# The sample's tile normalised and projected ahead of the prompt's last two tiles, instead of as the last one of the stage

## The chip, the cores and the metric

The kernel runs on one core of one Trainium2 chip. The metric is the device time of one execution in microseconds (us); a median of several executions is given with the lowest and the highest. The engines are named as in the profile: PE is the matrix engine (PEld its weight loads), DVE the vector engine, ACT the scalar engine, POOL the GpSimd engine, and SP the engine whose queue issues every DMA of this kernel.

## What is computed

One layer of a streaming encoder runs over two streams: a prompt of 2048 rows (16 tiles of 128 rows, numbered 0 to 15) and a sample of 32 rows (tile 16). Cut to what matters here:

```python
def _layer(x, c, pos, past_k, past_v, h0, lw):
    mod = silu(c) @ w_ada + b_ada
    sh1, sc1, g1, sh2, sc2, g2 = split(mod, 6)
    h = rmsnorm(x, ln1_g) * (1 + sc1) + sh1
    proj = h @ w_in                            # 1024 -> q 512 | k 128 | v 128 | u 512
    q = rope(rmsnorm(q per head), pos); k = rope(rmsnorm(k per head), pos)
    attn = banded attention of q, k, v         # the sample also reads cached k, v
    ssm_y, h_last = s5(u, h0, ...)             # state space layer over all rows of a stream
    g = gelu(ssm_y); ssm_o = g * sigmoid(g @ glu_w + glu_b)
    x = x + g1 * (concat(rmsnorm(attn), rmsnorm(ssm_o)) @ w_out)
    h2 = rmsnorm(x, ln2_g) * (1 + sc2) + sh2
    return x + g2 * ((silu(h2 @ w_gate) * (h2 @ w_up)) @ w_down), k rows, v rows, h_last
```

Both streams use the same weights, with their own conditioning vector, positions and past. Matrices are split into a high and a low float32r part, and a product is the sum of three matmuls (high by high, high by low, low by high).

## The kernel before

The kernel has four stages. Stage A normalises every tile of 128 rows, transposes it and multiplies it by `w_in`; stage B does the state space groups and the first attention tiles; stage C the rest of attention, the output projection and the residual; the last stage, by far the longest, is the feed-forward part. The change lies in stage A.

The kernel's text is a set of Python generators that are stepped in turn. A scheduler then orders the instructions of each engine, with the order of the text as their priority and a simulated time line to tell when each is ready; so instructions of different generators come out interleaved, and more finely than the text has them. Each engine, and SP's queue of DMA issues, then runs its list in order.

Stage A is the loop at lines 853 to 866. It goes through the tiles in pairs, `p` = 0 to 8: tiles (0, 1), (2, 3) up to (14, 15), and then tile 16 alone. For each pair it steps the projection of its tiles (`proj_steps`), and with every step of that

- one step, or two, of `x_steps(p + 1)`, the normalisation of the pair after it,
- one step of `wg`, which loads and splits the q, k and v columns of `w_in`, as long as there are any,
- two times in three a step of `bg1`, the conditioning vectors of the later stages (`ada_blocks`, tiles `adw`, `adh`, `adl`, `adp`, `adr`),
- one step of `bg2`, the tables and matrices of the state space layer (`ssm_background`; tiles `et`, `etb` on POOL, `m`, `mt`, `bv`, `spl` on DVE, `sph` on ACT, `kb` and `pbv` on PE).

`x_steps(p)` (lines 266 to 285) takes the row tiles `xg` of its pair. ACT squares and sums each (written into `hl` as scratch), POOL makes the inverse root (`rs`, two instructions), ACT scales the rows. Then `norm_steps` goes through the 8 blocks of 128 columns, one step for each: PE transposes the block of both tiles (`tr`), ACT applies scale and shift (`hf`), ACT or DVE makes the high part (`hh`) and DVE the low part (`hl`; for the sample both parts lie in `hh`). These results have two sets of buffers, so `x_steps(p + 1)` can begin only when the projection of pair `p - 1` has read its last block. For a pair it issues 16 transposes, for the sample 8 of 32 columns. At its end it issues the loads of later row tiles (`x_load`; `xg` has three buffers).

`proj_steps(j)` (lines 831 to 839) first does the u columns (`u_steps`: `ub`, copied to `us` and stored to `u_d`). Tiles 0 to 5 (`LATE`) store their normalised tile to `hT_d`, and their q, k and v are done at the start of stage B (`deferred`, tiles `dh` and `dl`). For all others `qkv_steps` follows: `qp` (512 columns), `kp` (256 columns), rotation on DVE (`qkvo`, `rb`) with the last addition on POOL, the per-head norm (`sq`, `ms`), and the stores to `qkv_d`; tile 15 and tile 16 also store their k and v rows to outputs (line 815). A prompt tile has 48 matmuls of 512 columns and 24 of 256. The sample has its high and low parts side by side as one stationary operand of 64 columns, so it has 32 of 512 and 16 of 256, and its two halves are added on DVE by `fold` (lines 126 to 129: a copy and an addition, for `ub`, `qp` and `kp`). Its `fold` results go to `qf`, which takes a buffer of `xg`.

When the loop is done, stage B opens. `ssm_batch` (lines 932 to 945) loads u rows 0 to 1023 (`ur`), has ACT rearrange them (`us`), loads rows 1024 to 2047 into the same single buffer `ur`, and then the sample's rows. The group steps load their matrices (`sm`, `ec`), and PE transposes u (`up`, lines 963 and 964).

Of the kernel before, what the change touches and what calls it, by code (L numbers as in the profile page):

```python
# [23 lines left out]
NT = NPT + 1  # L24
# [23 lines left out]
FLO = 576  # L48
CST = 2
QY = 2  # L50
LATE = [0, 1, 2, 3, 4, 5]
TILES = [*range(8, NPT), *range(8), NPT]
UNITS = [4, 5, 6, 7, 0, 1, 2, 3, 8]
# [20 lines left out]
def hybrid_kernel(  # L74
# [25 lines left out]
    def act(out, a, func=AF.Copy, **kw):  # L100
        A.activation(out, a, func, **kw)  # L101

    def f(a):
        return a.bitcast(F32)
# [37 lines left out]
    kp_d = dram.tile([16, G, 256], F32, name="kp_d")  # L142
    hT_d = dram.tile([len(LATE), 2, 128, KD * 128], F32, name="hT_d")
    sd_d = dram.tile([12, 4, 128, 512], F32, name="sd_d")
# [14 lines left out]
    def rpow(out, ss, n, eps, scr):  # L159
        ts(P, scr, ss, 1.0 / n, eps)  # L160
        tt(P, out, scr, mhalf[0:scr.shape[0]].to_broadcast(list(scr.shape)), ALU.pow)
# [23 lines left out]
    def qbank(nm="qp"):  # L185
        return pqs.tile([128, 512], F32, tag="q", name=nm)
# [21 lines left out]
    def advance(g, n=1):  # L208
        for _ in range(n):
            if next(g, None) is None:  # L210
                return
# [26 lines left out]
    def norm_steps(xs, rcol, s, hs, n, scv, shv, getbank, tmp):  # L238

        nt = len(xs)  # L240
        if rcol is not None:
            for j in range(nt):
                act(xs[j][0:n], xs[j][0:n], scale=rcol[0:n, j:j + 1])
        yield 1
        for k in range(KD):
            pb = getbank([128, nt, 128])
            for j in range(nt):
                PE.transpose(pb[:, j, 0:n], xs[j][0:n, k * 128:(k + 1) * 128], ident[0:n, 0:n])
            hf = tmp([128, nt, n])
            act(hf, pb[:, :, 0:n], AF.Identity, scale=scv[:, k, s:s + 1], bias=shv[:, k, s:s + 1])  # L250
            split(hs[0][:, 0:nt, k, 0:n], hs[1][:, 0:nt, k, 0:n], hf, V if k % 2 else A, V)
            yield 1

    xt, ht = {}, {}

    def x_load(j):
        if j >= NT:
            return
        x = px.tile([128, D], F32, tag="xg", name="xg", bufs=3)
        if j < NPT:  # L260
            SP.dma_start(x, x_prompt[0, j * 128:(j + 1) * 128])
        else:
            SP.dma_start(x[0:DEC], x_sample[0])
        xt[j] = x

    def x_steps(p):
        tl = [j for j in (2 * p, 2 * p + 1) if j < NT]
        xs = []
        hs = [px.tile([128, 2, KD, 128], F32R, tag=t, name=t, bufs=2) for t in ("hh", "hl")]
        rs = px.tile([128, 3, 2], F32, tag="rs", name="rs", bufs=2)  # L270
        for i, j in enumerate(tl):
            x = xt.pop(j)
            n = 128 if j < NPT else DEC
            act(hs[1][0:n, i].rearrange("p k n -> p (k n)"), x[0:n], AF.Square, accum_out=rs[0:n, 0, i:i + 1])
            xs.append(x)
            ht[j] = (hs[0][:, i], hs[1][:, i])
        if n < 128:
            ht[j] = (hs[0][:, 0, :, 0:2 * n], None)
            hs = [hs[0][:, :, :, i * n:i * n + n] for i in range(2)]
        nt = len(tl)  # L280
        rpow(rs[0:n, 1, 0:nt], rs[0:n, 0, 0:nt], D, EPS, rs[0:n, 2, 0:nt])
        yield 1
        yield from norm_steps(xs, rs[:, 1], 0 if n == 128 else 1, hs, n, sc1, sh1, tbank, partial(px.tile, dtype=F32, tag="hf", name="hf", bufs=3))
        for j in tl:
            x_load(j + 3)

    def ada_vectors(i, row, getbank):
        which, half = divmod(i, 2)
# [11 lines left out]
    def ada_first():  # L300
# [4 lines left out]
        for k in range(KD):  # L305
            if k == 3:
                for i in range(4):
                    SP.dma_start(rows[i][4:5], b_ada[0:1, i * 512:(i + 1) * 512])
            if k == 7:
                x_load(0)  # L310
                x_load(1)
                advance(xg)
            for i in (2, 3, 0, 1):
                wf = wq_tile("wqh" if k % 2 else "wql", 2 * (k // 2 % 2) * 2 + i, F32)[:, 0:512]
                wh = pz.tile([128, 512], F32R, tag="adfh", name="adfh", bufs=2)
                wl = pz.tile([128, 512], F32R, tag="adfl", name="adfl", bufs=2)
                SP.dma_start(wf, w_ada[0, k * 128:(k + 1) * 128, i * 512:(i + 1) * 512])
                split(wh, wl, wf, A, V)
                mm(acc[i], cst[:, k], wh, k == 0, False)
                mm(acc[i], cst[:, k], wl, False, k == KD - 1)  # L320
# [400 lines left out]

    wur = [px.tile([128, 4, 512], F32, tag=t, name="wur", bufs=2) for t in ("hh", "hl")]
    xg = x_steps(0)
    bg2 = ssm_background()
    ada_first()
# [33 lines left out]
    def product(dst, h, wh, wl, o, w):  # L759
        for k in range(KD):  # L760
            mm3(dst, h[0][:, k], h[1] and h[1][:, k], wh[k][:, o:o + w], wl[k][:, o:o + w], k == 0, k == KD - 1)
            if k % 2 and (w == 512 or k == 3) and k < KD - 1:
                yield 1
# [54 lines left out]
    def u_steps(j, h):  # L818
        n = 128 if j < NPT else DEC
        ub = qbank() if j in LATE else psu.tile([128, 512], F32, tag="ub", name="ub")  # L820
        yield from product(ub if n == 128 else ub[0:2 * n], h, [wuh[:, k] for k in range(KD)],
                           [wul[:, k] for k in range(KD)], 0, 512)
        yield 1
        us = psx.tile([128, 512], F32, tag="us", name="us")[0:n]
        if n < 128:
            fold(us, ub)
        else:
            cp(A, us, ub)
        SP.dma_start(u_d[j * 128:j * 128 + n], us)

    def proj_steps(j):
        h = ht.pop(j)
        if j in LATE:
            for i in range(2):
                SP.dma_start(hT_d[LATE.index(j), i], f(h[i]).rearrange("p k n -> p (k n)"))
        yield from u_steps(j, h)
        yield 1
        if j not in LATE:
            yield from qkv_steps(j, h)

    def deferred(i):
# [3 lines left out]
        yield 1  # L845
        yield from qkv_steps(LATE[i], h)

# [2 lines left out]
    ny = 0  # L850
    for _ in xg:
        pass
    for p in range((NT + 1) // 2):
        xg = x_steps(p + 1) if 2 * p + 2 < NT else iter(())
        for j in (2 * p, 2 * p + 1):
            if j >= NT:
                continue
            for _ in proj_steps(j):
                ny += 1
                advance(xg, 1 if j not in LATE else 2)  # L860
                advance(wg)
                if ny % 3:
                    advance(bg1)
                advance(bg2)
        for _ in xg:
            pass
# [473 lines left out]
    def c_norm(j):  # L1340
# [18 lines left out]
        V.tensor_reduce(sa[:, 0:n], sq.rearrange("p k n -> p n k"), AX.X, ADD)  # L1359
        for _ in range(QY):  # L1360
            yield 1
# [547 lines left out]
```

## Time and profile before

| what | value |
|---|---|
| median of 3 executions | 2328.24 us |
| lowest, highest | 2323.45, 2330.09 us |
| the profiled execution | 2332.55 us, of which its span is 2330.8 us |
| granted PE clock over the span | 0.968 |
| PE busy over the span | 2211.3 us |
| DVE, ACT, POOL busy over the span | 1718.3, 1261.2, 1256.3 us |

The profile is of one execution. Its page gives busy times over the span; its other views used here are windows (busy time of each engine in a stretch of time, with the number of instructions in brackets, the granted PE clock as a share of full speed, the busy share of the DMA engines and GB/s), groups of instructions by line (count, busy time, mean duration in ns, idle time before them), who waited for whom, and the timeline (start, duration, engine, line, instruction, and in square brackets the idle time before it and what ended it). Matmuls are pipelined: a row's duration is longer than the distance from one start to the next.

### The profile page before, as it was taken

To read this page: it belongs to the slowest core of one execution; us is meant where nothing else is said; L and a number is where in the kernel's file an instruction comes from. 1 tells how busy PE (TensorE), PEld (TensorE's weight loads), DVE (VectorE), ACT (ScalarE), POOL (GpSimd) and SP (SyncE) were. 2 spreads that over 40 slices of the span, in tenths; PEclk is the share of its full clock that TensorE was granted. 3 is DMA by queue.
4 is the path that set the end of the run, shared out by engine and by line. 5 is a ranking of instruction groups with operands and counts; after the bars stand their busy time and mean duration, and the time that the engine had idled before them with its cause. 6 is when DMAs were issued, how large, how long until landed. Compare 5 with 4: busy or idle time off the path is not lost.

```text
span 2330.8 us, 39040 instructions
## 1 busy us (share of the span) xinstructions
PE 2211.3 (95%) x13286; PEld 2055.1 (88%) x13286; DVE 1718.3 (74%) x2737; ACT 1261.2 (54%) x2544; POOL 1256.3 (54%) x1173
## 2 busy tenths in 40 slices
PE   7888898898899999999999998999999999999999
PEld 4576776786788888799999998999999989999998
DVE  6888874678777884766768779556677796677887
ACT  6655443555666655544445566444455754444664
POOL 1167775776366764578884136555521375565122
PEclk8899998898899999999999999999999999999999
DMA  7757676676323125457666644643365436534653
GB/s 232 264 169 239 192 219 205 196 232 200 102 75 93 55 69 174 150 174 219 209 200 213 184 142 154 180 122 111 101 199 170 132 110 183 147 97 120 199 164 125
DMA packets 429573, 380.12 MB, mean 163 GB/s; under 512 B 57327, under 2 KB 358987, under 8 KB 429373
## 3 DMA queue, kind: packets, MB, share of 16 engines
q1 hardware_dynamic: 429372, 377.63, 53.1%
q8 instruction: 104, 1.70, 0.3%
q14 instruction: 97, 0.79, 0.1%
HBM read 284.63 MB, written 92.91 MB: 162 GB/s over the span
## 4 chain that ended last, share of the span: by engine, by line
PE 63%; DVE 6%; ACT 2%; issue 2%; POOL 1%; DMA 1%; SPq 0%; DVEq 0%; POOLq 0%; ACTq 0%
PE fx L117 30%; PE fy L117 15%; PE fz L117 8%; PE co L117 5%; PE cb L117 1%; PE ob L117 1%; DVE wl L89 1%; PE pt L1070 1%; PE ft L1454 1%; ACT pbuf L101 1%; DVE ss L1332 1%; DVE bl L89 0%; PE fo L1721 0%; PE s L117 0%; DVE gl L89 0%
## 5 line engine op out<-in xcount | busy, mean ns | idle before, releaser
L89 DVE TENSOR_TENSOR wl<-wr,wh 128x512 fp32r<-128x512 f32 (+1 forms) x708 | 641.0, 921 | 252.2 <-ACT wh L101 248.9
L101 ACT ACTIVATE wh<-wr 128x512 fp32r<-128x512 f32 (+1 forms) x708 | 431.1, 617 | 552.7 <-PE fx L117 301.5
L117 PE MATMUL fx<-bh,wh 128*128 128x352 f32 (+1 forms) x1576 | 507.4, 322 | 6.2 <-DVE acc L98 3.8
L117 PE MATMUL fx<-bl,wh 128*128 128x352 f32 (+1 forms) x1576 | 506.4, 321 | 4.3 <-DVE bl L89 4.3
L117 PE MATMUL fx<-bh,wl 128*128 128x352 f32 (+1 forms) x1576 | 507.4, 322 | 0.0
L89 POOL TENSOR_TENSOR wr<-wr 128x512 f32<-128x512 f32 x256 | 388.0, 1525 | 185.6 <-DVE wl L89 138.9
L117 PEld LDWEIGHTS fx<-bh,wh 128*128 128x128 f32 x1576 | 298.1, 189 | 6.9 <-DVE acc L98 4.0
L117 PEld LDWEIGHTS fx<-bl,wh 128*128 128x128 f32 x1576 | 298.0, 189 | 5.2 <-DVE bl L89 5.2
L117 PEld LDWEIGHTS fx<-bh,wl 128*128 128x128 f32 x1576 | 297.6, 189 | 0.1
L89 POOL TENSOR_TENSOR c<-c,acc 128x352 f32<-128x352 f32 (+1 forms) x72 | 93.0, 1296 | 311.0 <-ACT c L101 293.2
L117 PE MATMUL fy<-bh,wh 128*128 128x352 f32 (+1 forms) x792 | 254.8, 322 | 1.1 <-DVE acc L98 0.8
L117 PE MATMUL fy<-bh,wl 128*128 128x352 f32 (+1 forms) x792 | 254.1, 321 | 0.0
L117 PE MATMUL fy<-bl,wh 128*128 128x352 f32 (+1 forms) x792 | 253.7, 320 | 0.0
L89 POOL TENSOR_TENSOR c<-c 128x352 f32<-128x352 f32 (+1 forms) x96 | 135.8, 1416 | 174.5 <-ACT wh L101 73.6
L117 PEld LDWEIGHTS fy<-bh,wh 128*128 128x128 f32 x792 | 149.6, 189 | 1.6 <-DVE acc L98 1.0
L117 PEld LDWEIGHTS fy<-bl,wh 128*128 128x128 f32 x792 | 149.4, 189 | 0.0
L117 PEld LDWEIGHTS fy<-bh,wl 128*128 128x128 f32 x792 | 149.0, 188 | 0.0
L89 DVE TENSOR_TENSOR bl<-q,bh 128x1408 fp32r<-128x1408 f32 (+3 forms) x85 | 140.7, 1660 | 5.1 <-ACT bh L101 5.1
L117 PE MATMUL fz<-bh,wl 128*128 128x352 f32 (+1 forms) x412 | 132.2, 324 | 4.5 <-DVE wl L89 4.5
L117 PE MATMUL fz<-bh,wh 128*128 128x352 f32 (+1 forms) x412 | 133.6, 325 | 1.0 <-ACT wh L101 0.9
L117 PE MATMUL fz<-bl,wh 128*128 128x352 f32 (+1 forms) x412 | 132.6, 322 | 0.0
L101 ACT ACTIVATE bh<-q 128x1408 fp32r<-128x1408 f32 (+3 forms) x85 | 108.5, 1284 | 17.4 <-DVE q L89 14.6
(388 smaller groups left out, 5135.3 us busy)
## 6 DMA issues: line engine op xcount, KB each, us to landing
wr<-in_w_gate_dram SPq DMA_DIRECT2D x132, 256.0 KB
wr<-in_w_up_dram SPq DMA_DIRECT2D x132, 256.0 KB
wr<-sd_d SPq DMA_DIRECT2D x96, 256.0 KB
wr<-in_w_down_dram SPq DMA_DIRECT2D x72, 256.0 KB
adw<-in_w_ada_dram SPq DMA_DIRECT2D x64, 256.0 KB
f_d<-c SPq DMA_DIRECT2D x88, 176.0 KB
sm<-sm_d SPq DMA_DIRECT2D x32, 448.0 KB
q<-f_d SPq DMA_DIRECT2D x16, 704.0 KB
```

Source lines behind the costliest of these rows:

```text
L89: e.tensor_tensor(out, a, b, op=op)
L101: A.activation(out, a, func, **kw)
L117: PE.matmul(out, lhsT, rhs, start=start, stop=stop, skip_group_check=more)
L1070: PE.transpose(pt[:, kb, i * 128:(i + 1) * 128], pbuf[:, kv * npair + i, kb * 128:kb * 128 + 128], ident)
L1332: V.tensor_reduce(ss[:, 0:n], sq[:, :, 0:n].rearrange("p k n -> p n k"), AX.X, ADD)
L1454: PE.transpose(pb[:, 128 * i:128 * i + m], x[0:m, k * 128:(k + 1) * 128], ident[0:m, 0:m])
```

## The change

The order of the tiles in stage A is now a list, `LINE` = 0 to 13, 16, 14, 15, and the grouping another, `PAIRS`: seven pairs of prompt tiles up to (12, 13), then the sample alone, then (14, 15). Row tiles are loaded in this order, `x_steps` takes its tiles from it, and the loop goes through the groups. So the sample is normalised while tiles 12 and 13 are projected, tiles 14 and 15 are normalised while the sample is projected, and they are projected last, with no normalisation beside them. No instruction is added or taken away.

```diff
+LINE = [*range(14), 16, 14, 15]
+PAIRS = [*((i, i + 1) for i in range(0, 14, 2)), (14,), (15, 16)]
...
-    def x_load(j):
-        if j >= NT:
+    def x_load(i):
+        if i >= NT:
             return
+        j = LINE[i]
...
     def x_steps(p):
-        tl = [j for j in (2 * p, 2 * p + 1) if j < NT]
+        tl = [LINE[i] for i in PAIRS[p]]
...
-        for j in tl:
-            x_load(j + 3)
+        for i in PAIRS[p]:
+            x_load(i + 3)
...
-    for p in range((NT + 1) // 2):
-        xg = x_steps(p + 1) if 2 * p + 2 < NT else iter(())
-        for j in (2 * p, 2 * p + 1):
-            if j >= NT:
-                continue
+    for p, pair in enumerate(PAIRS):
+        xg = x_steps(p + 1) if p + 1 < len(PAIRS) else iter(())
+        for j in (LINE[i] for i in pair):
             for _ in proj_steps(j):
```

## The prediction

> **What bounds the kernel now.** The page comes first.
>
> ```profile
> span 2330.8 us, 39040 instructions
> PE 2211.3 (95%) x13286; PEld 2055.1 (88%) x13286; DVE 1718.3 (74%) x2737; ACT 1261.2 (54%) x2544; POOL 1256.3 (54%) x1173
> ```
>
> PE is busy for 95% of the span, and the change takes no work from it. What it can move is PE's idle and slow time in stage A and at the border to stage B. So I cut that part into windows, at the first matmul of each tile (12, 13, 14, 16) and at the border; two short ones show the border more closely.
>
> ```profile
> 258.20:281.10 22.90, 20.52 (x110) 16.67 (x110) 14.42 (x22) 11.64 (x22) 19.24 (x24) 0.99 0.76 228
> 281.10:306.40 25.30, 21.74 (x110) 17.14 (x109) 24.64 (x37) 10.54 (x23) 21.85 (x23) 0.93 0.69 199
> 306.40:327.50 21.10, 21.10 (x108) 16.26 (x107) 16.58 (x28) 11.80 (x28) 18.83 (x22) 1.00 0.75 211
> 347.20:358.40 11.20, 11.20 (x58) 7.55 (x56) 6.36 (x11) 1.71 (x4) 5.75 (x7) 1.00 0.28 89
> 358.40:375.30 16.90, 9.33 (x37) 7.14 (x36) 5.68 (x12) 3.85 (x6) 6.82 (x9) 0.77 0.91 273
> 375.30:390.00 14.70, 11.79 (x56) 10.59 (x57) 6.80 (x13) 7.12 (x18) 9.70 (x11) 0.62 0.89 271
> 361.00:365.00 4.00, 4.00 (x11) 3.17 (x12) 1.39 (x3) 0.29 (x2) 2.96 (x5) 0.59 0.43 127
> 368.20:374.00 5.80, 0.40 (x4) 0.18 (x2) 0.73 (x2) 1.06 (x1) 0.00 (x0) 0.75 1.11 306
> ```
>
> The columns are length, then PE, PEld, DVE, ACT and POOL busy, PE clock, DMA share, GB/s. Three things are to be seen. In the window of tile 13 DVE is busy 24.64 of 25.30 us, and PE idles 25.30 - 21.74 = 3.56 us. With tile 14 and with the sample (347.20 to 358.40) PE never idles. Behind the sample comes the border: PE idles 16.90 - 9.33 = 7.57 us, and afterwards the clock is 0.62 for 14.70 us, while the DMA engines are about full (0.91, and 1.11 in the long gap). The border is told by the timeline:
>
> ```profile
> 358.21 0.28 PE L117 MATMUL kp<-wql,hh 128*64 128x256 f32 x1
> 360.85 0.77 PE L117 MATMUL qp<-wqh,dh 128*128 128x512 f32 x1 [1.38 <-DVE qf L89]
> 361.32 0.34 SPq L815 DMA_DIRECT2D out_dram<-qkvo  x1
> 361.70 0.59 SPq L939 DMA_DIRECT2D ur<-u_d  x1
> 367.19 0.56 SPq L939 DMA_DIRECT2D ur<-u_d  x1
> 368.49 0.42 SPq L815 DMA_DIRECT2D out_dram<-qkvo  x1
> 372.71 1.06 ACT L101 ACTIVATE us<-ur 128x1024 f32<-128x1024 f32 x1 [5.55 <-DMA ur<-u_d]
> 373.27 0.69 DVE L89 TENSOR_TENSOR qkvo<-qp,tabg 128x512 f32<-128x512 f32 x1 [10.88 <-DMA out_dram<-qkvo]
> 373.82 0.69 PE L963 MATMUL up<-cpk,us 128*128 128x128 f32 x2 [5.40 <-ACT us L101]
> 375.32 0.58 PE L117 MATMUL kp<-wqh,dh 128*128 128x256 f32 x1 [0.81 <-ACT sq L101]
> ```
>
> Two chains end together there. One: the sample's last matmul, its v rows out at 361.32, behind that on SP's queue the first `ur` load, the second `ur` load, ACT's copy at 372.71, PE at 373.82. The other: the sample's second output store at 368.49, which holds the single `qkvo` buffer until 373.27, then DVE, ACT, PE at 375.32. Only what shortens both is gained. Tile 15, which becomes the last, has the same stores in this profile:
>
> ```profile
> 347.11 0.28 PE L117 MATMUL kp<-wqh,hl 128*128 128x256 f32 x1
> 349.17 0.34 SPq L815 DMA_DIRECT2D out_dram<-qkvo  x1
> 354.08 0.42 SPq L815 DMA_DIRECT2D out_dram<-qkvo  x1
> ```
>
> **The change, part by part.**
>
> *The border.* The sample's v rows go out 361.32 - (358.21 + 0.28) = 2.83 us behind its last matmul, tile 15's 349.17 - (347.11 + 0.28) = 1.78 us behind: 1.05 us sooner. The second store comes at 10.0 us with the sample (368.49 - 358.49) and at 6.69 with tile 15: 3.3 us sooner. The lesser decides: **-1.05 us**. PE's wait of 1.38 us at 360.85 is no gain of its own, since PE stands at 373.82 whenever it came there. Least: nothing, if another DMA holds `ur` as long. Most: the whole border, below.
>
> *The window of tiles 12 and 13.* The normalisation beside them becomes the sample's instead of that of two full tiles. First the low and high parts of tiles 14 and 15 (all but one of them in the window of tile 13), then those of the sample, 306 to 347, then what PE waited for longest in the window of tile 13:
>
> ```profile
> L89 DVE TENSOR_TENSOR hl<-hf,hh 128x256 fp32r<-128x256 f32 x8 | 5.1, 641 | 0.0
> L110 DVE CAST hh<-hf 128x256 fp32r<-128x256 f32 x4 | 3.7, 928 | 0.0
> ...
> L89 DVE TENSOR_TENSOR hh<-hf,hh 128x32 fp32r<-128x32 f32 x8 | 2.0, 264 | 0.2
> L110 DVE CAST hh<-hf 128x32 fp32r<-128x32 f32 x4 | 1.6, 410 | 0.0
> ...
> PE adv L117 <- DVE adr L372: 1.7, 1, 1.7
> PE kb L117 <- DVE spl L89: 1.3, 1, 1.3
> ```
>
> DVE there loses 8.8 us and gets 3.6: 5.2 us are freed on the engine that PE waits for. Between nothing (the background's loads set the pace instead) and all 3.56 us of PE's idle time I take half, 1.8 us. The clock adds to it: the window ran at 0.93, so 25.30 x 0.07 = 1.8 us were lost beside 3.56 of idling, half a microsecond for each. **-2.7 us**, bounds 0 and -5.3.
>
> *The window of the sample, now between tiles 13 and 14.* Tiles 14 and 15 are now normalised beside 13 short steps. The rows for how long that took, for the pair from tile 12's first matmul on, and for the sample from tile 14's:
>
> ```profile
> 258.18 0.52 PE L117 MATMUL ub<-wuh,hh 128*128 128x512 f32 x1
> 259.49 1.06 ACT L101 ACTIVATE hl<-xg 128x1024 fp32r<-128x1024 f32 x1
> 270.86 2.19 ACT L101 ACTIVATE xg<-xg,rs 128x1024 f32<-128x1024 f32 x2 [2.79 <-POOL rs L89]
> 272.67 0.38 PE L248 MATMUL tr<-cpk,xg 128*128 128x128 f32 x2
> 301.70 0.41 DVE L89 TENSOR_TENSOR hl<-hf,hh 128x256 fp32r<-128x256 f32 x1
> ...
> 306.37 0.39 PE L117 MATMUL ub<-wuh,hh 128*128 128x512 f32 x1
> 306.60 0.40 PE L117 MATMUL ub<-wul,hh 128*128 128x512 f32 x1
> 307.88 1.05 ACT L101 ACTIVATE hl<-xg 32x1024 fp32r<-32x1024 f32 x1
> 316.95 0.31 PE L248 MATMUL tr<-cpk,xg 32*128 32x32 f32 x2
> ```
>
> PE's work first. A matmul of 512 columns starts 0.23 us behind another (306.37, 306.60), one of 256 in half that. The sample has 32 x 0.23 + 16 x 0.115 = 9.2 us, tile 14 48 x 0.23 + 24 x 0.115 = 13.8 of its 21.10. The other 7.3 us are background, some 1 of it the sample's transposes; the background goes by steps and both tiles have 13, so 6.3 us lie beside the sample too. The pair's 16 transposes, two in 0.38, add 3.0. That is 18.5 us. The first transposes came 272.67 - 258.18 = 14.5 us after the pair's start with two tiles (10.6 with one, 306.37 to 316.95), so the first blocks of tile 14 are ready before PE wants them: the lower bound is no wait. On DVE the same steps hold the 16.58 us of tile 14's window, less half of the sample's 3.6, plus 8.8, plus the folds:
>
> ```profile
> 347.20:362.00 14.80, 1.78 (x3) 0.96 0.38 133
> ```
>
> (this window holds the three copies of `fold` alone; each has an addition of its size behind it, so some 3.5 us). That makes 27.1 us, less the 5.2 us of background that run ahead in tile 13's window: 21.9 against PE's 18.5, at most 3.4 us of waiting. I take the middle of 0 and 3.4, 1.7, and half as much for the clock: **+2.6 us**. Past it, `ub`, `kp` and `qkvo` of the sample meet those of tile 14 at least a product later, and `qf` takes the sample's own row buffer, free by then; I count them at nothing, and a single `ub` read late by DVE would cost one fold, 1.4 us. The sample's store to `u_d` and the row loads are the same issues on SP in another place; loads come a whole group ahead of their use.
>
> *The windows of tiles 14 and 15.* They lose the sample's 8 transposes, which tile 12's and 13's get: nothing in sum. DVE (16.58 of 21.10) and ACT have room there already, so less work beside them gains nothing.
>
> Sum: -1.05 - 2.7 + 2.6 = -1.15 us. Against the profiled execution's 2332.55 us that is 2331.4; its time lies 4.3 us over the median of the runs shown, so I put the difference on the median: 2328.24 - 1.15 = **2327.1 us**. About 0.3%, 7.0 us, is what a measurement of this kernel can tell from no change.
>
> **The rivals.**
>
> *Slower: DVE doesn't keep up beside the sample.* If the background doesn't run ahead while tiles 12 and 13 are done (it may wait for its weight loads), DVE has 27.1 us against PE's 18.5: 8.6 us of waiting, half as much again for the clock, 12.9, less 1.05: 2340.1. For it speaks that tiles 14 and 15 took until 302.11 - 258.18 = 43.9 us after their pair's start, while PE will want their last block 18.5 + 24 x 0.23 = 24 us after the sample's start. Against it: with tile 12 and 13 nothing wanted them sooner. It decides from the point at which the last `hl` comes over 24 + 7 = 31 us after the sample's first matmul.
>
> In this profile, 1.38 us of idling were followed by 4.00 us at a clock of 0.59. The Trainium skill, "TensorE: Matmul & The Clock Gate", "What's actually happening", says that the clock halves only after an idle window of about 3.4 us. By that rule the scattered waits of this rival would cost no clock, and it would give 2328.24 + 8.6 - 1.05 = 2335.8; the row doesn't bear the rule out.
>
> *Faster: the border closes.* If the scheduler sees the `ur` loads ready sooner, now that no fold holds them, and puts them ahead of tile 15's store, both of PE's losses there can go: 7.57 us of idling and 14.70 x 0.38 = 5.6 us at the low clock, 13.2 in all: 2315. For it: DMA stands at a share of 0.28 before the border and is full behind it. Against: the second `ur` load needs the first one's buffer, took 5.5 us from issue to ACT's copy, and shares full DMA engines with the matrix loads; and tile 15's store stands on the same queue at the same place. It decides when the first `ur` load goes out before the last matmul of stage A.
>
> *No effect.* The scheduler moves single steps past each other anyway, and DVE's background is the same in sum; what tile 13's window gains, the sample's loses, and the border stays DMA's: 2328.2.
>
> **How the numbers follow.** The forecast and the case of no effect, which differ by 1.15 us, have 0.60 together (0.35 and 0.25). The faster rival, in whole or by more than half its price, has 0.23: full DMA engines speak against the whole of it. The slower one has 0.17: it needs DVE's background to stand still in the stretch that is relieved. The range takes the bounds of the parts, -5.3 - 1.05 (2321.9) and +5.1 (3.4 x 1.5), and reaches from there until about one in ten is left on each side: 2318 to 2338. The chances are those of the cases: faster 0.23, same 0.60, slower 0.17.
>
> **What would show it.** Border: the v store of tile 15 about 1.8 us behind stage A's last matmul, the first `ur` load right behind it, and DVE's first `qkvo` of stage B no longer released by an output store. Tile 13: DVE below 24 of 25 us and PE idling less than 3.56. Sample: PE's idle time between its first matmul and tile 14's last `ub`, expected 0 to 3.4 us, released by DVE `hl`. The forecast is wrong if this last wait exceeds 7 us, if the border's idle time falls below half of 7.57, or if a later stage changes by more than stage A does.

## The result and the profile after

The changed kernel takes 2357.80 us (median of 3, 2356.17 to 2361.48) against 2328.24: ratio 1.0127, 95% interval 1.0109 to 1.0145. It is slower by 29.6 us, where 2327.1 in a range of 2318 to 2338 was forecast. Its profiled execution took 2356.17 us, the shortest of its three, and before's 2332.55, more than any of its three; so the profiles differ by 23.6 us only. The page of the changed kernel:

```profile
span 2354.4 us, 39040 instructions
PE 2215.8 (94%) x13286; PEld 2055.5 (87%) x13286; DVE 1722.8 (73%) x2737; ACT 1263.3 (54%) x2544; POOL 1249.7 (53%) x1173
```

The instructions are the same in number and kind; PE is busy for 4.5 us more (its granted clock is 0.966 for 0.968) and idle for 19 us more. Three points of PE's timeline part the span: the first `qp<-wqh,dh` (stage B begins), the one `gsp` matmul (state space groups done, stage C begins) and the first `fx` (feed-forward begins).

| | before | after | difference |
|---|---|---|---|
| stage A, to the first deferred `qp` | 360.8 us | 376.6 us | +15.8 |
| from there to `gsp` (B) | 225.8 | 197.6 | -28.2 |
| from `gsp` to the first `fx` (C) | 363.9 | 401.0 | +37.1 |
| from there to the end | 1380.3 | 1379.2 | -1.1 |

So stage A loses 15.8 us, and B and C, of which nothing was changed, lose 8.9 in sum. The windows of the changed kernel that answer to those shown of before: tile 12, tile 13, the sample, tile 14, tile 15 and the border (length, then PE, PEld, DVE, ACT, POOL busy, PE clock, DMA share, GB/s).

```profile
263.00:285.40 22.40, 20.58 (x109) 15.41 (x107) 18.79 (x30) 13.62 (x28) 19.41 (x25) 1.00 0.69 191
285.40:316.20 30.80, 22.01 (x90) 15.27 (x89) 13.24 (x23) 9.41 (x21) 17.85 (x29) 0.86 0.72 204
316.20:331.40 15.20, 15.17 (x81) 10.63 (x82) 12.44 (x20) 5.68 (x13) 13.21 (x11) 0.94 0.54 138
331.40:350.90 19.50, 16.11 (x69) 12.48 (x68) 17.27 (x33) 9.21 (x21) 7.57 (x8) 0.82 0.63 192
350.90:373.10 22.20, 22.08 (x122) 18.87 (x120) 6.28 (x12) 2.76 (x6) 12.33 (x16) 1.00 0.57 178
373.10:390.00 16.90, 8.35 (x30) 6.43 (x31) 4.39 (x8) 4.24 (x8) 6.89 (x7) 0.79 0.85 257
```

The hole is in tile 13's window: PE idles 30.80 - 22.01 = 8.79 us (3.56 before), and no engine is full there, DVE no more than the others (13.24 of 30.80). PE, DVE and ACT all wait, so the reason has to stand on a queue. The timeline of the changed kernel, POOL, PE, DVE, ACT and SP's queue of DMA issues put together in order of time:

```profile
276.53 1.71 POOL L91 TENSOR_TENSOR qkvo<-qkvo,ms 128x640 f32<-128x640 f32 x1
...
301.46 1.24 SPq L683 DMA_DIRECT2D tf<-kp_d  x3
305.44 0.51 SPq L626 DMA_DIRECT2D e_d<-et  x1
...
308.00 1.50 SPq L348 DMA_DIRECT2D adw<-in_w_ada_dram  x3
...
310.03 0.50 SPq L815 DMA_DIRECT2D qkv_d<-qkvo  x1
310.57 0.45 SPq L832 DMA_DIRECT2D u_d<-us  x1
311.77 0.63 ACT L103 ACTIVATE adh<-adw 128x512 fp32r<-128x512 f32 x1 [9.05 <-DMA adw<-in_w_ada_dram]
312.44 2.63 DVE L91 TENSOR_TENSOR adl<-adw,adh 128x512 fp32r<-128x512 f32 x3 [8.43 <-ACT adh L103]
312.46 0.80 PE L119 MATMUL adp<-adh,cst 128*128 128x512 f32 x1 [7.89 <-ACT adh L103]
315.58 0.60 ACT L103 ACTIVATE us<-ub 128x512 f32<-128x512 f32 x1 [1.44 <-DMA u_d<-us]
315.59 0.68 DVE L91 TENSOR_TENSOR qkvo<-qp,tabg 128x512 f32<-128x512 f32 x1
316.23 0.69 PE L119 MATMUL ub<-wuh,hh 128*64 128x512 f32 x1
317.15 0.63 PE L119 MATMUL ub<-wuh,hh 128*64 128x512 f32 x1
318.00 0.40 PE L119 MATMUL ub<-wuh,hh 128*64 128x512 f32 x1
```

Tile 11's `qkvo` was finished by POOL at 276.53 + 1.71 = 278.24 us. Its store went out at 310.03, **31.8 us later**. SP was not asleep: from 277.94 on it issued 49 other DMAs, whose rows add up to 26.7 us, and it stood from 302.7 to 305.44 for `et`. The store simply has a late place on SP's list: it is the 373rd DMA issued there, and the 324th in before. (The expectations below speak of 60 issues and of place 292; they count otherwise.) There is one `qkvo` buffer, so tile 12's rotation could not begin before this store had read it.

But the store is not the only late entry. Ahead of it stand three loads of `adw`, the weights of the background (308.00), and behind it tile 12's store to `u_d` (310.57). The waits that ended last are for the loads: ACT waited 9.05 us for `adw`, DVE 8.43 and PE 7.89 us for the `adh` that ACT makes of it. DVE did that work, then a step of the background, and went on to tile 12's rotation at 315.59 without another wait. The store to `u_d` held the single `us` and so the single `ub`: ACT's copy came at 315.58, and the sample's first `ub` at 316.23. Tile 13's `kp`, which needs the `kp` bank that the rotation reads, came at 323.2, behind the sample's `u`. So loads and stores of SP's list are late together, and this timeline alone doesn't say which of them costs how much.

In before the same store:

```profile
273.08 1.25 POOL L89 TENSOR_TENSOR qkvo<-qkvo,ms 128x640 f32<-128x640 f32 x1
274.65 0.45 SPq L812 DMA_DIRECT2D qkv_d<-qkvo  x1
279.73 0.68 DVE L89 TENSOR_TENSOR qkvo<-qp,tabg 128x512 f32<-128x512 f32 x1
```

It lay 0.3 us. No `qkv_d` store of before lay over 5 us in stage A.

### The profile page after: what moved, and what is told of

Read it like the earlier page. It is cut to its first block, busy times and chain, and to the rows that moved or that the text cites. A ratio compares the mean times of both kernels' runs of the same rounds, so it can differ in the third digit from the quotient of the medians.

```text
span 2354.4 us, 39040 instructions
## 1 busy us (share of the span) xinstructions
PE 2215.8 (94%) x13286; PEld 2055.5 (87%) x13286; DVE 1722.8 (73%) x2737; ACT 1263.3 (54%) x2544; POOL 1249.7 (53%) x1173
## 4 chain that ended last, share of the span: by engine, by line
PE 63%; DVE 7%; issue 3%; POOL 2%; ACT 1%; DMA 1%; SPq 0%; DVEq 0%; POOLq 0%; ACTq 0%
PE fx L119 30%; PE fy L119 15%; PE fz L119 8%; PE co L119 4%; PE cb L119 2%; PE ob L119 1%; DVE wl L91 1%; PE pt L1071 1%; DVE bl L91 1%; DVE gl L91 1%; PE ft L1455 0%; DVE st L1055 0%; PE fo L1722 0%; DMA wr<-in_w_up_dram 0%; DVE ss L1333 0%
```

## The experiments

The kernels were run in five sets, each with before's runs on the same chip (medians 2328.24 to 2331.45 us). The ratios are to these, so kernels of different sets are compared by their ratios. "Lag" is tile 11's store behind POOL's last multiply; A ends with the first deferred `qp`, B + C with the first `fx`, all in the profiled execution. In `stores_after`, `store_first_after` and `before_lists_store_first` stage B begins with `up` instead, at 392.2, 361.4 and 362.1 us.

| kernel | median us | ratio, 95% interval | lag | A ends | B + C |
|---|---|---|---|---|---|
| before | 2328.24 | 1 | 0.3 | 360.8 | 589.7 |
| after | 2357.80 | 1.0127 (1.0109 to 1.0145) | 31.8 | 376.6 | 598.6 |
| own_buffer_after | 2351.72 | 1.0085 (1.0055 to 1.0115) | 46.2 | 377.2 | 591.0 |
| own_buffer_before | 2326.98 | 0.9986 (0.9973 to 0.9999) | 0.9 | 363.3 | 581.8 |
| stores_after | 2368.31 | 1.0162 (1.0131 to 1.0192) | 4.8 | 399.5 | 584.6 |
| stores_before | 2348.02 | 1.0068 (1.0049 to 1.0087) | 8.6 | 388.0 | 578.6 |
| store_first_after | 2333.77 | 1.0013 (1.0000 to 1.0026) | 1.0 | 374.5 | 570.9 |
| store_first_before | 2345.02 | 1.0062 (1.0049 to 1.0075) | 0.0 | 365.1 | 594.9 |
| store_on_pool_after | 2348.17 | 1.0070 (1.0051 to 1.0088) | none on SP | 380.4 | 586.7 |
| products_in_order | 2337.35 | 1.0033 (1.0023 to 1.0043) | 32.3 | 379.5 | 573.0 |
| stage_a_after_lists_before | 2346.45 | 1.0072 (1.0060 to 1.0085) | 31.8 | 374.6 | 584.5 |
| stage_a_before_lists_after | 2348.02 | 1.0084 (1.0071 to 1.0097) | 0.7 | 359.9 | 610.0 |
| store_first_lists_before | 2336.27 | 1.0033 (1.0021 to 1.0046) | 0.0 | 363.9 | 588.9 |
| stage_a_before_lists_in_order | 2321.18 | 0.9972 (0.9961 to 0.9983) | 0.0 | 360.9 | 575.1 |
| own_store_lists_before | 2337.56 | 1.0031 (1.0017 to 1.0044) | 0.4 | 364.2 | 588.4 |
| before_lists_store_first | 2336.63 | 1.0019 (1.0008 to 1.0030) | 0.6 | 376.8 | 576.9 |
| store_first_lists_in_order | 2327.71 | 0.9986 (0.9974 to 0.9997) | 1.2 | 364.5 | 580.3 |

**The shared buffers.** Three normalised groups, (12, 13), the sample and (14, 15), share two sets of `hh` and `hl`. This gives the sample a buffer of its own:

```diff
-        hs = [px.tile([128, 2, KD, 128], F32R, tag=t, name=t, bufs=2) for t in ("hh", "hl")]
-        rs = px.tile([128, 3, 2], F32, tag="rs", name="rs", bufs=2)
+        hs = ([px.tile([128, 2, KD, 128], F32R, tag=t, name=t, bufs=2) for t in ("hh", "hl")] if tl[0] < NPT
+              else [px.tile([128, 1, KD, 128], F32R, tag="hs", name="hs", bufs=1)] * 2)
+        rs = px.tile([128, 3, 2], F32, tag="rs", name="rs", bufs=1)
```

> The changed order, but the sample's normalised parts get a buffer of their own (hs, 4 KB a partition; the little rs tile goes from two buffers to one to make room), so that hh and hl serve pairs of tiles alone. Theory of the buffers (tiles 14/15 can be normalised only when tile 13's projection has read its last block, because three groups share two buffers): hh<-hf of tiles 14/15 starts before tile 13's last kp, PE's waits for hl and hh between the sample and tile 14 go, and stage A, 15.8 us longer in the changed kernel than before (first deferred qp at 376.6 against 360.8 us), gets at least 8 us of that back: 2350 us or less. Rival, PE's list (background adp matmuls ahead of tile 13's kp, held by adw loads that stand behind the e_d stores on SP): the buffers change nothing that matters, stage A stays within 4 us of +15.8, 2354 to 2360. Theory of the later stages (the compiler's order there changed by itself): B and C still 5 us or more over before's 589.7.

> Before's order with the same own buffer for the sample (and the same one-buffer rs). It is the control: no wait of before is for hh or hl beside the sample, so by the theory of the buffers stage A moves by less than 3 us and the time is 2325 to 2331. If the later stages lose time whenever the order of instructions is worked out anew, whatever the edit, this kernel too gets 5 us or more longer in B and C although the sample stands last: 2333 to 2340.

Stage A ends at 377.2 with it, as late as without, and the store lies even longer, 46.2 us: the theory of the buffers falls. The total gained something (a ratio of 1.0085 for 1.0127); in the profiled execution that stands in B and C, 7.6 us shorter than in the changed kernel. The median of 2351.72 lies in the range of neither theory, and B and C (591.0) are not 5 us over before's 589.7, as the third had it. The control stayed within its 2325 to 2331, but by two moves of opposite sign: stage A ended 2.5 us later, B + C were 7.9 us shorter. It was the first sign that B and C move by themselves.

**The e_d stores.** Both orders, with `e_d` issued by POOL:

```diff
-            SP.dma_start(e_d[2 * q + par, :, :, 0:257], src)
-            SP.dma_start(e_d[2 * q + par, :, :, 257:262], src[:, :, 0:5])
+            P.dma_start(e_d[2 * q + par, :, :, 0:257], src)
+            P.dma_start(e_d[2 * q + par, :, :, 257:262], src[:, :, 0:5])
```

> The changed order, but the e_d stores go out on POOL's queue, where their source is made, not on SP's. Theory of PE's list: SP no longer stands behind e_d, adw arrives in time, the 7.9 us wait of an adp matmul for adh at 312 us and the 3.4 us one for adl go, and stage A gets 7 us or more of its 15.8 back: 2343 to 2351. Theory of the buffers: the 7.9 us wait may go, but tile 14 then waits for hl as long; stage A gets less than 4 us back: 2353 to 2359.

> Before's order with the e_d stores on POOL's queue: the control. Stage A of before has no PE wait over 5.9 us and none for adh; by both theories it moves by less than 3 us (2325 to 2331), unless the issue of 64 DMAs on POOL holds up its ropes. If later stages lose time with any new order of instructions, B and C are 5 us or more longer here too.

Both theories missed. Tile 11's long lag went, but an issue takes POOL 0.64 us, 64 of them 41 us, and stage A became 23 us (after; 16 by the first `up`) and 27 us (before) longer. PE's wait for `adh` fell to 0.8 us. A second cost was added that is larger than the one under test, so the pair tells nothing of it.

**The one store.** The stores to `qkv_d` get a high priority in the text. The scheduler makes all lists anew with it, so more than this store can move:

```diff
-        SP.dma_start(qkv_d[j * 128:j * 128 + n], o)
+        with tc.high_priority():
+            SP.dma_start(qkv_d[j * 128:j * 128 + n], o)
```

> The changed order, and each tile's store of its rotated q, k, v (qkv_d<-qkvo) is put on SP's list with high priority; nothing else. In the changed kernel tile 11's store was ready at 278.2 us (end of POOL's last multiply) and issued at 310.0, 31.8 us later, behind 60 other issues that the compiler's list has ahead of it; there is one qkvo buffer, so tile 12's rope (315.6), its kp's readers and tile 13's kp (323.2) waited for it; in before the same store lay 0.3 us. The list now has it at place 256 as before's, not 292. Theory of SP's list (this one store makes stage A's loss): no lag over 6 us, the hole at 300 to 320 us (PE busy 11.2 us of 20) goes, first deferred qp at 366 us or sooner, 2345 us or less. Theory of the short sample (a 64-column tile between pairs can't cover tile 14/15's normalisation, whatever the lists): first deferred qp still at 370 or later, 2350 or more.

> Before's order with the same high priority on the stores: the control. No store of before lies over 5 us; first deferred qp 358 to 364 us, 2323 to 2334 us by both theories.

In `store_on_pool_after` the line is `P.dma_start(qkv_d[j * 128:j * 128 + n], o)`.

> The changed order with the qkv_d stores issued by POOL, whose multiply is the last to write qkvo, so that they pass SP's list altogether. Theory of SP's list: as with the high priority, first deferred qp at 366 us or sooner and 2345 us or less. The compiler's list has 80 score matmuls of the attention ahead of gsp here, as in before (64 in the changed kernel): if it is that count that makes B and C 9 us longer, they are back within 3 us of before's 589.7; if not, over 594.

The changed order with the store in its place comes to a ratio of 1.0013 for 1.0127, and is equal to before within 0.26%. The store went out at 274.13, 1.0 us after its data. But "first deferred `qp` at 366 or sooner" missed: in this kernel stage B begins with `up`, at 361.4, and the deferred products come later. The control is worse than a miss: before's own order, where the store was never late, became 0.62% **slower** by the same line, with B + C at 594.9. So a total of one kernel proves nothing about the store; the lists of the later stages changed with each of these edits. With the store on POOL both expected numbers were missed (380.4 for 366, 2348 for 2345): POOL itself was 7 us late with tile 11 by then, its multiply ended at 285.4. Its 80 score matmuls ahead of `gsp` came with 586.7, within 3 us of before's 589.7 as the count had it; the next kernel refutes the count all the same.

**PE's order at the hole.** From tile 12 on, each product on PE's list stands behind the one before it in the text:

```diff
     def product(dst, h, wh, wl, o, w):
         for k in range(KD):
-            mm3(dst, h[0][:, k], h[1] and h[1][:, k], wh[k][:, o:o + w], wl[k][:, o:o + w], k == 0, k == KD - 1)
+            with tc.issue_after(last[0]) if last else ExitStack():
+                mm3(dst, h[0][:, k], h[1] and h[1][:, k], wh[k][:, o:o + w], wl[k][:, o:o + w], k == 0, k == KD - 1)
+            if pin[0]:
+                last[:] = [nc.cur_bb.bb.instructions[-1]]
```

> The changed order, and from tile 12 on PE's list has the products in the order of the program: tile 13's kp ahead of the sample's u, which the compiler had put the other way round. SP's list still has tile 11's store at place 292. Theory of SP's list: the store lies over 25 us again, tile 13's kp still waits for tile 12's rope, the hole stays, first deferred qp at 373 us or later, 2350 or more. Theory of PE's list (it is the swap of kp and the sample's u that costs): first deferred qp at 369 us or sooner, 2346 us or less.

The store lay 32.3 us, and stage A ended at 379.5: the order of `kp` and `u` is not the cause. SP's list, late in the same way here (`adw` at 309.36, the store at 311.39, PE waiting 8.3 us for `adh`), fits, as that theory had it. The kernel's total fell, though: 2337 and not 2350. Stage A was 2.9 us worse than in the changed kernel, and B + C 25.6 us shorter, with 64 score matmuls ahead of `gsp` as there. Two causes, then, and neither can be read from a total.

**Stage A and the later lists apart.** From the end of stage A on, both programs issue the same instructions, in lists of their own. So one kernel's scheduled order of them can be laid on the other, engine by engine, with constraints of order that add no waits of their own:

```diff
+    last = list(nc.cur_bb.bb.instructions)[-17940:]
...
+        own = [i for i in last if str(i.engine) == engine and type(i).__name__ != "BassTilePoolBoundary"]
+        at, was = 0, None
+        for step in steps:
+            at += step
+            if was is not None:
+                tc.add_manual_dep(own[at], was.name, info, reason="order")
+            was = own[at]
```

> Stage A as the compiler orders it in the changed kernel; from the end of stage A on, every engine and every DMA queue gets its instructions in the very order that they have in before (17,882 order constraints, no other edit; both programs issue the same instructions there). If the loss lies in stage A alone, with tile 11's store 30 us late on SP and PE's hole: first FFN row at 975, 2354 to 2359 us. If it lies in the lists of the later stages alone and stage A's lateness is made good behind it: 950, 2328 to 2334. If both add up (376.6 us to the first deferred qp, and before's 589.7 us from there on): 966, 2346 to 2350.

> The other way round: before's order in stage A, and from its end on the lists of the changed kernel. Loss in stage A alone: 2328 to 2334 us. Loss in the later lists alone: 2354 to 2359. Both added (360.8 and 598.6 us): first FFN row at 959, 2338 to 2343.

> The changed order with the high priority on the qkv_d stores (tile 11's store 1 us after its data, no hole), and before's lists from the end of stage A on. Against the first kernel of this call, which has the same later lists and the late store, it prices the late store itself. If the late store costs what stage A shows: 12 to 18 us faster than that kernel, 2328 to 2335. If its lateness is made good behind it: within 4 us of that kernel.

> Before's order in stage A, and from its end on the lists of the kernel products_in_order, in which B and C took 573.0 us (before 589.7). If that length belongs to the lists: 360.8 + 573.0 + 1381.5, first FFN row at 934, 2315 to 2320 us, faster than before though the sample stands last. If it belongs to the late start (379.5 us, when more work lay ready): 2326 to 2334.

The traces bear the exchange out: in the first two kernels each engine's and SP's list agrees entry by entry with the one kernel in stage A and with the other behind it. Each half alone costs: the changed stage A with before's lists 0.72%, before's stage A with the changed lists 0.84%. Together they are 1.27%, a little less than the sum, 1.56; by the order in which they are added, stage A is worth 0.43 to 0.72% (10 to 17 us) and the lists 0.55 to 0.84% (13 to 20 us), each give or take some 0.15%. The median of `stage_a_after_lists_before` came out as the sum of the milestones had it (2346 to 2350); its profiled run, with `fx` at 959.1 for 966, was the quickest of five. `stage_a_before_lists_after` came at 2348.0, between the sum's 2338 to 2343 and the 2354 of "lists alone", in the range of neither.

`stage_a_after_lists_before` and `store_first_lists_before` have the same later lists, and their texts differ in the priority of the `qkv_d` stores alone: 2346.45 - 2336.27 = 10.2 us, with intervals that don't overlap. That is less than the 12 to 18 expected and more than the 4 of "made good behind it". It is not the price of one late store, though. With the priority the scheduler made stage A's lists anew too, SP's from the 194th issue on and PE's from the 664th matmul: tile 12's store to `u_d` left at 297.38 instead of 308.27, and loads of `adw` at 298.72, 303.40 and 304.46, where the other kernel issued none from 294.01 to 305.69. So 10.2 us is what stage A's order with these late entries costs against an order with the store in its place; the shares of the store, of the loads and of the rest of the order were not separated. The window of 300 to 350 us shows the same, in this order: before, after, the changed stage A with before's lists, and that one with the store in place.

```profile
300.00:350.00 50.00, 48.13 (x237) 38.42 (x238) 35.06 (x61) 20.57 (x48) 35.53 (x42) 0.93 0.71 207
```

```profile
300.00:350.00 50.00, 37.78 (x167) 26.04 (x166) 35.33 (x58) 19.88 (x43) 29.61 (x32) 0.83 0.59 166
```

```profile
300.00:350.00 50.00, 37.57 (x167) 26.27 (x166) 36.02 (x59) 18.22 (x39) 30.81 (x33) 0.83 0.61 173
```

```profile
300.00:350.00 50.00, 43.55 (x221) 32.34 (x220) 39.53 (x63) 19.02 (x42) 31.71 (x37) 1.00 0.65 185
```

The matmuls done are what to look at: 237, 167, 167, 221. With the store late 70 are missing from the window, and the clock is 0.83; with the store in place 16 are missing and the clock is 1.00.

How far the later lists carry their length with them is seen by taking all kernels with one set of lists:

| lists from | stage A of | B us | C us | `up` to `fx` us |
|---|---|---|---|---|
| before | before | 225.8 | 363.9 | 582.5 |
| before | after; store first; store first and own buffer | 221.6; 225.2; 225.1 | 362.9; 363.7; 363.3 | 576.0; 580.2; 579.8 |
| after | after; before | 197.6; 207.4 | 401.0; 402.6 | 591.6; 602.1 |
| products_in_order | its own; before; store first | 186.4; 189.5; 191.9 | 386.6; 385.6; 388.4 | 567.3; 568.7; 572.2 |
| store_first_after | its own; before | 183.1; 186.7 | 387.8; 390.2 | 584.0; 591.6 |

C's length goes with the list to within 3 us, whatever ran in stage A; B's moves by up to 9.8 us with stage A, and `up` to `fx` by up to 10.5. The longest wait in C goes with the list too. Who waited for whom on PE in stage C (us in total, times, longest): before, after, and before's stage A with the changed lists:

```profile
PE pt L1070 <- POOL pbuf L89: 0.7, 2, 0.4
```

```profile
PE pt L1071 <- POOL pbuf L91: 10.0, 3, 4.6
PE s L119 <- DVE att L112: 3.5, 2, 2.5
PE kb L1040 <- DVE tl L91: 2.8, 1, 2.8
```

```profile
PE pt L1071 <- POOL pbuf L91: 10.1, 3, 4.6
PE kb L1040 <- DVE tl L91: 3.3, 1, 3.3
```

With the changed lists PE waits three times for a normalised block of attention weights (`pbuf`), 10.0 and 10.1 us in sum. With before's lists it is 0.7. That is the part of the difference between these two sets that has a name, and it is no general reason: the fastest kernel, before's stage A with the lists of `products_in_order`, waits in C for `pbuf` too, 4.2 us for POOL and 6.3 for ACT. The rest is spread over many small waits, and what in the order makes one set of lists good is open.

Before's stage A with the lists of `products_in_order` is 0.28% faster than before (0.17 to 0.39), 1 us over the 2315 to 2320 expected: another order of the same instructions, the sample still last, and the fastest kernel of the study. It also shows that 64 score matmuls ahead of `gsp` do no harm.

**What is left of the change.** Three more pairs; `own_store_lists_before` joins the own buffer, the high priority and before's lists.

> The changed order with the high priority on the stores and with the sample's own buffer hs (one rs tile), and before's lists from the end of stage A on: store_first_lists_before plus the buffer. Theory of the shared buffers (they make what is left of the loss, 7.6 us over before): PE's wait of 1.65 us for tile 14's hl goes, first deferred qp at 361 us or sooner (363.9 without the buffer), 2328 to 2332 us. If the sharing costs nothing once the store is in place: within 3 us of 2336, first deferred qp 362 to 366.

> Before's order in stage A, and from its end on the lists of store_first_after, in which B and C took 570.9 us from the first deferred qp on (up came before it there, at 361.4 us, so that the length from up on is 584.0; before's is 582.5). If the later lists alone set the length from up on: first FFN row at 952, 2328 to 2334 us. If they set it from the first deferred qp on: 932, 2311 to 2317.

> The changed order with the high priority on the stores, and from the end of stage A on the lists of products_in_order. If stage A and the later lists add up: 7.5 us (lists) below store_first_lists_before's 2336.3, 2326 to 2331 us, the sample's change then costs the same 7 us over stage_a_before_lists_in_order (2321.2) as it does with before's lists. If they don't add up: outside that.

With the store in place and the later lists the same, the change still costs 0.33% (0.21 to 0.46) with before's lists, and 0.14% with those of `products_in_order` (0.9986 against 0.9972). Some 3 of these 7 us are lost by the end of stage A (363.9 for 360.8); what costs them, and where the rest goes, is open. The own buffer takes tile 14's wait for `hl` away, and nothing is won (1.0031 for 1.0033), as the second theory had it; a longer wait, for the background's `adh`, stands on PE's list there. First without the own buffer, then with it, on PE's timeline:

```profile
321.72 0.50 PE L119 MATMUL ub<-wuh,hl 128*128 128x512 f32 x1 [1.65 <-DVE hl L91]
```

```profile
328.44 0.51 PE L119 MATMUL adp<-adh,cst 128*128 128x512 f32 x1 [4.22 <-ACT adh L103]
```

`before_lists_store_first` agrees with "from `up` on" by `fx`, 953.7 for 952; its median is 2.6 us over the 2334 that went with it. The 2327.71 of `store_first_lists_in_order` lies in its 2326 to 2331. But before ran 2 us slower on that chip than on the one of the forecast, and the intervals behind 0.33% and 0.14% overlap; so stage A and lists add up there to within some 4 us, and no closer.

## Why the prediction was wrong

**What failed first: "The sample's store to `u_d` and the row loads are the same issues on SP in another place".** SP's queue was counted at nothing because the issues were the same. But the scheduler works out SP's list anew, and entries that the change doesn't touch got late places on it: three loads of `adw`, tile 11's store to `qkv_d` and tile 12's to `u_d`. PE, DVE and ACT stood 7.89 to 9.05 us for the loads. Price: 10.2 us for stage A's order with these late entries against one with the store in its place; that the store alone makes it is not shown. In all three builds of the changed order that schedule by themselves and leave the stores as they are (after, own_buffer_after, products_in_order) tile 11's store lies 31.8 to 46.2 us; in before and in own_buffer_before 0.3 and 0.9. Why the scheduler's simulated time line puts it and the loads there isn't shown.

**What failed second: the sum stops at the end of stage A.** "The scheduler moves single steps past each other anyway" was used as a reason for no effect. The later stages' lists were new as well, and cost 13 to 20 us. The prediction's last sentence named a later stage that changes by more than stage A as what would make it wrong, and gave it neither a price nor a chance. Controls that leave the sample last moved by -0.14% and +0.62% with their new lists; a spread of that size, 3 us down and 14 up, belonged into the range.

**The window of tiles 12 and 13 (-2.7).** DVE was relieved, as said: 13.24 us of 30.80, where "below 24 of 25" was asked for. PE's idle time rose to 8.79 us all the same. The relieved engine was not the one that ended the wait there: it waited itself, 8.43 us for `adh`. That "the background's loads set the pace instead", the reason given for the lower bound of nothing, is what came, and it cost time.

**The window of the sample (+2.6).** In the changed kernel PE idles 0.03 us beside the sample and 19.50 - 16.11 = 3.39 us beside tile 14, against "at most 3.4"; but the wait is for `adl`, not for `hl`, so the size came out by luck. In `store_first_lists_before` PE does wait for `hl`, 1.65 us, where 1.7 was taken; there the mechanism was right and the wait's size too, but not the half added for the clock, which is 1.00 from 300 to 350 us.

**The border (-1.05).** It gave nothing: PE idles 16.90 - 8.35 = 8.55 us in the window from 373.10 on, 7.57 in before's of the same length. Tile 15's v store went out 3.6 us behind the end of stage A's last matmul (372.98), not 1.78. The condition of the faster rival came true, and not its gain. On the changed kernel's timeline:

```profile
368.30 0.59 SPq L940 DMA_DIRECT2D ur<-u_d  x1
376.59 0.34 SPq L818 DMA_DIRECT2D out_dram<-qkvo  x1
376.62 0.80 PE L119 MATMUL qp<-wqh,dh 128*128 128x512 f32 x1 [3.64 <-ACT qkvo L103]
384.88 0.44 PE L964 MATMUL up<-cpk,us 128*128 128x128 f32 x2 [0.90 <-ACT us L103]
389.45 0.58 PE L119 MATMUL kp<-wqh,dh 128*128 128x256 f32 x1 [4.14 <-ACT sq L103]
```

The first `ur` load left 4.4 us before stage A's last matmul began (372.70), and `up` waited only 0.90 us (5.40 before). But the other of the two chains, store, `qkvo`, `sq`, `kp`, held PE for 4.14 us (0.81 before), and the first deferred `qp` waited 3.64 us for ACT's copy of tile 15's `kp` into `qkvo`, where it waited 1.38 us for the sample's `fold` before. So the idle time is spread otherwise over the three waits, and nothing of it is gained.

**The slower rival** had the right sign, and its condition came true: the background waited for its weight loads while tiles 12 and 13 were done. What it made of that was wrong. It put the loss on DVE beside the sample, and the loss fell on PE itself in tile 13's window. The last `hl` came 32.4 us after the sample's first matmul at 316.23, past the 31 us from which the rival was to decide:

```profile
348.20 0.40 DVE L91 TENSOR_TENSOR hl<-hf,hh 128x256 fp32r<-128x256 f32 x1
```

But PE idled 0.03 us beside the sample, DVE was busy for 13.24 of 30.80 us where the time was lost, and with one more buffer for the parts, which hold `hl` back, nothing measurable was won.

## What to carry to other kernels

Where a scheduler makes the lists, a moved step is a new list for every queue: look for loads that engines wait for, and for results that are ready, whose entries stand late on a DMA queue, above all where a single buffer waits for such a store. Don't judge such a change by one total: lay one kernel's lists on the other's later stages, or what a new order does by itself (here up to 0.8%) is taken for the effect of the change. And it pays to try other orders of the same instructions: one of them gained 0.28% with no change of the work.

## What the runs showed of the hardware

A DMA issue takes its queue about half a microsecond (49 on SP in 26.7 us) and 0.64 us on POOL, so 49 places on a list are some 26 us, by estimate from these rows. After PE's wait of 7.89 us its matmuls of 512 columns lasted 0.60 to 0.80 us, and 0.40 again from 318.00 on: 5.5 us after it had begun again at 312.46. The Trainium skill, "TensorE: Matmul & The Clock Gate", "What's actually happening", has the full clock back after some 3.4 us of sustained work. Here 5.5 us passed, with a wait of 0.23 us among them (ended at 313.49), so this stretch doesn't test that figure. In `store_first_lists_before`, where PE's waits are short, the clock is 1.00 over the whole window of 300 to 350 us.
